# Grouped softmax: tiles of three rows in a ring of four, and one broadcast multiply per row in place of eight scalings

## The chip, the cores and the metric

The kernel runs on one core of one Trainium2 chip. The metric is the device time of that core in microseconds (us), as the median of repeated executions. Beside it stands one execution taken by the hardware profiler, which gives the trace that the profile is read from; its span runs from the first to the last instruction, and its time is a little longer than its span.

## The reference

The input `x` is 4 x 4096 x 4352 in float32. Each row of 4352 values is cut into eight groups of 544, and a softmax is taken over every group:

```python
x_g = x.reshape(B, N, 8, 544)
x_g = x_g - x_g.max(axis=-1, keepdims=True)
exp = np.exp(x_g)
out = exp / exp.sum(axis=-1, keepdims=True)
```

Each value is read once and written once: 285.2 MB come in and 285.2 MB go out, and each element sees one maximum, one exponential with its sum, and one multiply.

## The kernel before, in words

The 16,384 rows lie over 128 partitions, so that each partition handles 128 of them. From here on "row" means one such slot: 128 partitions x 4352 elements, 2.23 MB. `R = 2` rows make a tile (4352 KB), there are 64 tiles, and `NT = 6` buffers hold them in a ring, 12 rows in all. A partition's rows of one tile are adjacent in memory, so that each partition's share of a transfer is one run of 34,816 bytes. The work is done in place: a tile's buffer receives the load, is overwritten by the exponentials and by the scaled values, and is the source of the store.

Three queues work side by side, ordered by semaphores written out by hand:

- SyncE (SP) issues all loads (line 115). From the seventh tile on it first waits until the store out of the same buffer is done (line 114).
- VectorE (DVE) takes, for each row, the negated maxima of the eight groups in one reduction (line 70), and later the reciprocals of the eight sums (line 75) and the eight multiplies, one for each group (line 79). Its order is: maximum of row n+1, then scaling of row n (lines 131 to 134). The first row of a tile waits for the landing of that tile (line 68).
- ScalarE (ACT) computes eight exponentials per row with the sums taken along (line 88), each followed in the trace by a short read of its accumulator. It also issues the stores (line 100).

When a store is issued is set by `LAG = 2`: at tile j, ACT waits for `seen`, which VectorE gives as it takes the landing of tile j, and issues the store of tile j-2 (lines 102 to 108). A tile that is computed waits in its buffer until the second tile after it has landed. The last two stores come without that delay.

The middle of both compute engines' programs is a loop with ten turns of six tiles; the loop heads are placed at a fixed slot of an instruction fetch block (lines 53 to 56). At the end SP waits for the last store of each buffer (lines 116 and 117).

Of the kernel before, what the change touches and what calls it, by code (L numbers as in the profile page):

```python
# [1 line left out]

# [5 lines left out]


@with_exitstack  # L10
def kernel(
    ctx: ExitStack,
    tc: tile.TileContext,
    x: bass.AP,
    out: bass.AP,
):
    nc = tc.nc
    G = 8
    P = 128
    R = 2  # L20
    NT = 6
    S = R * NT
    LAG = 2
    xf = x.flatten_outer_dims()
    of = out.flatten_outer_dims()
    N, D = xf.shape
    Dg = D // G
    nt = N // (P * R)
    turns = (nt - LAG) // NT
    rest = LAG + turns * NT  # L30
    assert rest == nt - 2
    f32 = mybir.dt.float32
    X = mybir.AxisListType.X
    Exp = mybir.ActivationFunctionType.Exp
    xt = xf.rearrange("(t p r) d -> t p (r d)", p=P, r=R)
    ot = of.rearrange("(t p r) d -> t p (r d)", p=P, r=R)
    turn_out = of[:turns * S * P, :].rearrange("(u b p r) d -> u b p (r d)", b=NT, p=P, r=R)

    landed = [tc.alloc_semaphore(f"landed{b}") for b in range(NT)]
    stored = [tc.alloc_semaphore(f"stored{b}") for b in range(NT)]  # L40
    seen = tc.alloc_semaphore("seen")
    max_done = tc.alloc_semaphore("max_done")
    exp_done = tc.alloc_semaphore("exp_done")
    rec_done = tc.alloc_semaphore("rec_done")
    scaled = tc.alloc_semaphore("scaled")

    ctx.enter_context(tc.tile_critical(no_gpsimd_drain=True))  # L47
    bufs = [ctx.enter_context(nc.sbuf_tensor(f"xt{b}", [P, R * D], f32)) for b in range(NT)]
    mx = ctx.enter_context(nc.sbuf_tensor("mx", [P, S, G], f32))
    sm = ctx.enter_context(nc.sbuf_tensor("sm", [P, S, G], f32))  # L50
    rs = ctx.enter_context(nc.sbuf_tensor("rs", [P, S, G], f32))

    def loop(engine):

        return nc.Fori(
            0, turns, engines=OrderedEngineSet([engine.engine]), head_slot={engine.engine: 0})

    def take(engine, sem, n=1):
        engine.sem_inc(sem, -n).wait_op(sem, n, "sem-ge")  # L59

    def row(s):
        b, r = divmod(s, R)
        return bufs[b][:, r * D:(r + 1) * D].rearrange("p (g d) -> p g d", g=G)

    def vector_max(n):
        s = n % S
        if s % R == 0:
            take(nc.vector, landed[s // R], 16)
            nc.vector.sem_inc(seen, 1)
        nc.vector.reduce_max(out=mx[:, s, :], in_=row(s), axis=X, negate=True).then_inc(max_done, 1)  # L70

    def vector_scale(n):
        s = n % S
        take(nc.vector, exp_done)
        nc.vector.reciprocal(out=rs[:, s, :], in_=sm[:, s, :]).then_inc(rec_done, 1)  # L75
        take(nc.vector, rec_done)
        xr = row(s)
        for g in range(G):
            i = nc.vector.tensor_scalar_mul(  # L79
                out=xr[:, g, :], in0=xr[:, g, :], scalar1=rs[:, s, g:g + 1])  # L80
        i.then_inc(scaled, 1)

    def scalar_exp(n):
        s = n % S
        take(nc.scalar, max_done)
        xr = row(s)
        for g in range(G):
            i = nc.scalar.activation(  # L88
                out=xr[:, g, :],
                in_=xr[:, g, :],  # L90
                func=Exp,
                bias=mx[:, s, g:g + 1],
                scale=1.0,
                accum_out=sm[:, s, g:g + 1],
            )
        i.then_inc(exp_done, 1)

    def store(b, target):
        take(nc.scalar, scaled, R)
        nc.scalar.dma_start(out=target, in_=bufs[b][:, :]).then_inc(stored[b], 16)  # L100

    def scalar_tile(j, *targets):

        take(nc.scalar, seen)
        for r in range(R):
            if r < len(targets):
                store((j - LAG + r) % NT, targets[r])
            scalar_exp(j * R + r)


    for t in range(nt):
        b = t % NT
        if t >= NT:
            nc.sync.wait_ge(stored[b], 16 * (t // NT))
        nc.sync.dma_start(out=bufs[b][:, :], in_=xt[t]).then_inc(landed[b], 16)
    for b in range(NT):
        nc.sync.wait_ge(stored[b], 16 * ((nt - b + NT - 1) // NT))


    nc.scalar.preload_act_table(Exp)  # L120
    for j in range(LAG):
        scalar_tile(j)
    with loop(nc.scalar) as u:
        for b in range(NT):
            scalar_tile(LAG + b, turn_out[u, b])
    scalar_tile(nt - 2, ot[nt - 4])
    scalar_tile(nt - 1, ot[nt - 3], ot[nt - 2])
    store((nt - 1) % NT, ot[nt - 1])


    def vector_rows(lo, hi):
        for n in range(lo, hi):
            vector_max(n + 1)
            vector_scale(n)

    vector_max(0)
    vector_rows(0, LAG * R)
    with loop(nc.vector):
        vector_rows(LAG * R, LAG * R + S)
    vector_rows(rest * R, nt * R - 1)  # L140
    vector_scale(nt * R - 1)


# [1 line left out]
_INS = ['x']  # L145
_OUTS = [((4, 4096, 4352), 'float32')]


# [23 lines left out]
```

## Time and profile before

| | us |
|---|---|
| median of 9 runs | 1330.17 |
| lowest and highest | 1329.98, 1332.93 |
| profiled execution, its own time | 1330.27 |
| its span | 1328.5 |
| VectorE busy | 1041.7 |
| ScalarE busy | 764.4 |

The page cuts the span into 40 equal slices and gives for each the busy tenths of every engine and of the 16 DMA engines, with the GB/s that they moved. Its groups name a line, an engine and an operation, then output and input with their shapes, the count, the busy time in us with the mean of one in ns, and behind the second bar the idle time ahead of them and what ended it. Queue 1 carries the loads, queue 10 the stores. In a timeline each line has start, duration (or, where several of a kind are merged, the time from the first to the end of the last), engine, line and count.

### The profile page before, as it was taken

Reading aid. Unit: us, or ns where it says so; the run is one execution under the profiler, and the core shown is the slowest. Engines: PE = TensorE matmul, PEld = TensorE weight load, DVE = VectorE, ACT = ScalarE, POOL = GpSimd, SP = SyncE. Lnnn points to the kernel's source line nnn. Section 1 sums busy time; section 2 is a strip of 40 time slices with the busy share of each in tenths; the row PEclk is TensorE's granted clock in tenths of the full one; section 3 lists DMA queues with packets and bytes.
Section 4 is the critical chain, followed back from the end, with each engine's and each line's share of the span. In section 5 each row is a group of like instructions: output and inputs, shape, how many; then the busy total and the mean of one; then the engine's idle time right before and its main releaser. Section 6 shows DMA issues by size and latency. Waiting matters only on the chain. (4 is left out here: it accounts for less than half of the span.)

```text
span 1328.5 us, 4328 instructions
## 1 busy us (share of the span) xinstructions
DVE 1041.7 (78%) x1280; ACT 764.4 (58%) x2049; POOL 0.2 (0%) x4
## 2 busy tenths in 40 slices
DVE  5899987877877878778787787877878778787781
ACT  3677755655556556565565655655556555565551
POOL 0000000000000000000000000000000000000000
DMA  9999999999999999999999999999999999999997
GB/s 403 418 435 436 434 433 426 434 435 436 436 432 428 433 434 436 436 433 428 432 435 435 436 435 427 431 435 436 435 435 428 432 433 436 436 435 429 430 433 328
DMA packets 18439, 570.49 MB, mean 429 GB/s; under 512 B 2048, under 2 KB 2048, under 8 KB 2048
## 3 DMA queue, kind: packets, MB, share of 16 engines
q1 hardware_dynamic: 9216, 285.22, 49.8%
q10 hardware_dynamic: 9216, 285.22, 49.7%
q14 instruction: 7, 0.06, 0.0%
HBM read 285.21 MB, written 285.21 MB: 429 GB/s over the span
## 5 line engine op out<-in xcount | busy, mean ns | idle before, releaser
L88 ACT ACTIVATE xt<-xt,mx 128x544 f32<-128x544 f32 x1024 | 751.2, 735 | 534.3 <-ACTq L59 534.3
L70 DVE TENSOR_REDUCE mx<-xt 128x8 f32<-128x4352 f32 x128 | 599.2, 4682 | 238.4 <-DVEq L59 235.5
L79 DVE TENSOR_SCALAR xt<-xt,rs 128x544 f32<-128x544 f32 x1024 | 434.1, 498 | 19.2
L88 ACT ACTIVATION_READ_ACCUMULATOR xt<-xt,mx 128x1 f32 x1024 | 191.1, 187 | 0.0
L75 DVE RECIPROCAL rs<-sm 128x8 f32<-128x8 f32 x128 | 24.7, 193 | 4.2 <-DVEq L59 4.2
L120 ACT ACT_TABLE_LOAD x1 | 1.3, 1283 | 0.9 <-SPq L47 0.9
L156 POOL MEMSET const-bfloat16-1.0<- 128x1 bf16 x1 | 0.1, 101 | 0.0
L156 POOL MEMSET const-uint8-127<- 128x1 uint8 x1 | 0.1, 101 | 0.0
L156 POOL MEMSET const-float32-0.0<- 128x1 f32 x1 | 0.1, 98 | 0.2 <-issue 0.2
L156 POOL MEMSET const-float32-1.0<- 128x1 f32 x1 | 0.1, 98 | 0.0
## 6 DMA issues: line engine op xcount, KB each, us to landing
xt<-in_x_dram SPq DMA_DIRECT2D x64, 4352.0 KB, 30.2
out_dram<-xt ACTq DMA_DIRECT2D x64, 4352.0 KB, 51.2
```

The costliest lines, as they stand in the source:

```text
L70: nc.vector.reduce_max(out=mx[:, s, :], in_=row(s), axis=X, negate=True).then_inc(max_done, 1)
L75: nc.vector.reciprocal(out=rs[:, s, :], in_=sm[:, s, :]).then_inc(rec_done, 1)
L79: i = nc.vector.tensor_scalar_mul(out=xr[:, g, :], in0=xr[:, g, :], scalar1=rs[:, s, g:g + 1])
L88: i = nc.scalar.activation(out=xr[:, g, :], in_=xr[:, g, :], func=Exp, bias=mx[:, s, g:g + 1], scale=1.0, accum_out=sm[:, s, g:g + 1],)
L120: nc.scalar.preload_act_table(Exp)
L156: nc = _bacc.Bacc("TRN2", target_bir_lowering=False, num_devices=1)
```

## The change

Tiles become three rows (`R = 3`, 6528 KB) in a ring of four buffers (`NT = 4`), so that the ring still holds 12 rows. 128 rows make 42 tiles of three and a last one of two, 43 in all. The first tile is loaded by three transfers of one row each, each with its own semaphore; the others by one.

The delay of the stores goes: `seen` and `LAG` are gone, and ACT issues the store of tile t right after the exponentials of the first row of tile t+1. Near the end the order is written out: VectorE scales the last row of tile 41 ahead of the maximum of tile 42's first row, and ACT issues the store of tile 41 ahead of the exponentials of that row.

The eight multiplies of a row become one `tensor_tensor` over 4352 elements, whose second input repeats each reciprocal along its group. The loops have ten turns of four tiles, with no slot named for their heads. The final waits follow the order of the stores.

```diff
-    R = 2
-    NT = 6
+    R = 3
+    NT = 4
     S = R * NT
-    LAG = 2
...
+    nr = N // P
+    nt = -(-nr // R)
+    last_rows = nr - (nt - 1) * R
+    turns = (nt - 2) // NT
...
+    first = [tc.alloc_semaphore(f"first{r}") for r in range(1, R)]
-    seen = tc.alloc_semaphore("seen")
...
-    def loop(engine):
-
-        return nc.Fori(
-            0, turns, engines=OrderedEngineSet([engine.engine]), head_slot={engine.engine: 0})
...
         if s % R == 0:
             take(nc.vector, landed[s // R], 16)
-            nc.vector.sem_inc(seen, 1)
+        elif n < R:
+            take(nc.vector, first[n - 1], 16)
...
-        for g in range(G):
-            i = nc.vector.tensor_scalar_mul(
-                out=xr[:, g, :], in0=xr[:, g, :], scalar1=rs[:, s, g:g + 1])
-        i.then_inc(scaled, 1)
+        nc.vector.tensor_tensor(
+            out=xr,
+            in0=xr,
+            in1=rs[:, s, :].unsqueeze(2).to_broadcast([P, G, Dg]),
+            op=mybir.AluOpType.mult,
+        ).then_inc(scaled, 1)
...
-    def scalar_tile(j, *targets):
-
-        take(nc.scalar, seen)
-        for r in range(R):
-            if r < len(targets):
-                store((j - LAG + r) % NT, targets[r])
-            scalar_exp(j * R + r)
+    def store(t, target):
+        take(nc.scalar, scaled, R if t < nt - 1 else last_rows)
+        nc.scalar.dma_start(out=target, in_=tile_of(t)).then_inc(stored[t % NT], 16)
...
+    x0 = xf[:P * R, :].rearrange("(p r) d -> p r d", r=R)
+    for r in range(R):
+        nc.sync.dma_start(out=bufs[0][:, r * D:(r + 1) * D], in_=x0[:, r, :]).then_inc(
+            first[r - 1] if r else landed[0], 16)
+    for t in range(1, nt):
         if t >= NT:
-            nc.sync.wait_ge(stored[b], 16 * (t // NT))
-        nc.sync.dma_start(out=bufs[b][:, :], in_=xt[t]).then_inc(landed[b], 16)
-    for b in range(NT):
-        nc.sync.wait_ge(stored[b], 16 * ((nt - b + NT - 1) // NT))
+            nc.sync.wait_ge(stored[t % NT], 16 * (t // NT))
+        nc.sync.dma_start(out=tile_of(t), in_=dram(xf, t)).then_inc(landed[t % NT], 16)
+    for t in range(nt - NT, nt):
+        nc.sync.wait_ge(stored[t % NT], 16 * (t // NT + 1))
...
+    scalar_exp(0)
+    with nc.scalar.Fori(0, turns) as u:
+        for t in range(NT):
+            for n in range(t * R + 1, t * R + R + 1):
+                scalar_exp(n)
+            store(t, turn_out[u, t])
+    for n in range(turns * S + 1, nr):
+        if n == (nt - 1) * R:
+            store(nt - 2, dram(of, nt - 2))
+        scalar_exp(n)
+        if n == (nt - 2) * R:
+            store(nt - 3, dram(of, nt - 3))
+    store(nt - 1, dram(of, nt - 1))
...
+    lead = R - 1
     vector_max(0)
-    vector_rows(0, LAG * R)
-    with loop(nc.vector):
-        vector_rows(LAG * R, LAG * R + S)
-    vector_rows(rest * R, nt * R - 1)
-    vector_scale(nt * R - 1)
+    vector_rows(0, lead)
+    with nc.vector.Fori(0, turns):
+        vector_rows(lead, lead + S)
+    vector_rows(lead + turns * S, (nt - 1) * R - 1)
+    vector_scale((nt - 1) * R - 1)
+    vector_max((nt - 1) * R)
+    vector_rows((nt - 1) * R, nr - 1)
+    vector_scale(nr - 1)
```

## The prediction

> **What bounds the kernel now.** I read the page first: the slices, the queues, the groups.
>
> ```profile
> DVE  5899987877877878778787787877878778787781
> ACT  3677755655556556565565655655556555565551
> DMA  9999999999999999999999999999999999999997
> q1 hardware_dynamic: 9216, 285.22, 49.8%
> q10 hardware_dynamic: 9216, 285.22, 49.7%
> L88 ACT ACTIVATE xt<-xt,mx 128x544 f32<-128x544 f32 x1024 | 751.2, 735 | 534.3 <-ACTq L59 534.3
> L70 DVE TENSOR_REDUCE mx<-xt 128x8 f32<-128x4352 f32 x128 | 599.2, 4682 | 238.4 <-DVEq L59 235.5
> L79 DVE TENSOR_SCALAR xt<-xt,rs 128x544 f32<-128x544 f32 x1024 | 434.1, 498 | 19.2
> ```
>
> The DMA engines are busy in every slice; loads and stores take equal halves, 99.5% together. VectorE idles 238.4 us, nearly all ahead of its maxima, that is, waiting for landings. So transfers set the time, and a change can act in three places only: the time of a pass of bytes, the start, and the end, if the DMA then lacks work. The chain of work is no help: it stops at VectorE's last multiplies at 1303, while the stores run on.
>
> Next, the timelines: SP's loads, ACT's first store, the last two stores, and VectorE at the end.
>
> ```profile
> 609.66 41.47 SPq L115 DMA_DIRECT2D xt<-in_x_dram  x3
> 1228.63 21.01 SPq L115 DMA_DIRECT2D xt<-in_x_dram  x2
> 48.92 5.47 ACTq L100 DMA_DIRECT2D out_dram<-xt  x1
> 1289.02 0.34 ACTq L100 DMA_DIRECT2D out_dram<-xt  x1
> 1303.59 0.34 ACTq L100 DMA_DIRECT2D out_dram<-xt  x1
> 1177.18 4.68 DVE L70 TENSOR_REDUCE mx<-xt 128x8 f32<-128x4352 f32 x1 [4.10 <-DVEq L59]
> 1181.78 0.19 DVE L75 RECIPROCAL rs<-sm 128x8 f32<-128x8 f32 x1
> 1182.12 3.40 DVE L79 TENSOR_SCALAR xt<-xt,rs 128x544 f32<-128x544 f32 x8
> 1185.44 4.68 DVE L70 TENSOR_REDUCE mx<-xt 128x8 f32<-128x4352 f32 x1
> 1280.58 4.68 DVE L70 TENSOR_REDUCE mx<-xt 128x8 f32<-128x4352 f32 x1 [4.10 <-DVEq L59]
> ```
>
> Loads go out every 20.57 us in the middle ((41.47 - 0.33)/2) and every 20.68 us at the end. In that time two rows come in and two go out, so a pass of one row in one direction costs 20.68/4 = 5.17 us; I use 5.16. VectorE's starts give 4.60 for a maximum, 0.34 from reciprocal to multiply and 3.32 for eight multiplies, 8.26 a row. Last, the end in windows (busy time of the three engines with counts, clock, DMA share, GB/s):
>
> ```profile
> 1315.00:1320.00 5.00, 0.00 (x0) 0.00 (x0) 0.00 (x0) 1.00 0.90 390
> 1320.00:1325.00 5.00, 0.00 (x0) 0.00 (x0) 0.00 (x0) 1.00 0.11 49
> ```
>
> The DMA runs full until 1319.4; in finer windows single packets of one or two slower engines follow until 1325.0, and the span ends 3.5 us later. The DMA thus never lacks work, and the reason is a store backlog. Call the rows landed but not yet stored the **lead**. The load issued at 1249.3 needed store 57, done some 1.8 us earlier (as 1325.0 stands to SP's release at 1326.8): 116 rows stored, and 124.9 landed, since VectorE takes tile 62 at 1259.90. Lead 8.9. At the last landing, 1280.0, 8.9 rows make 46 us of stores, to 1326 (seen: 1325.0), and the last store, issued at 1303.59, joins a queue that still has work.
>
> **The Trainium skill.** "VectorE: DVE Perf Modes", the perf-mode tier table, gives float32 `tensor_scalar` two elements per cycle and `tensor_tensor` one. The trace agrees for the first: 3.32/8 = 415 ns for 544 elements, below the 567 ns that one per cycle at 0.96 GHz needs; it has none of the second. "Vector Engine (DVE) Microarchitecture Reference", measured stream behaviour, gives 1.0417 ns per column plus about 75 ns: 4.61 us for 4352, and the maximum shows 4.60. "DMA: Bandwidth & Descriptors", queues, rings and completion order, says that an engine takes turns between its queues packet by packet, as the equal halves show; where 436 GB/s comes from, same page, has 27.2 GB/s per port, so that 34,816 bytes need 1.280 us, against 20.68/16 = 1.2925 here.
>
> **The change, part by part.**
>
> *Multiply.* Eight for 3.32 us become one of 4.61 us (estimate from that slope; it can't be less, one-element rate being the operation's best). A row costs VectorE 4.60 + 0.34 + 4.61 = 9.55, a tile 28.7. Its DMA period is 6 x 5.16 = 31.0, so 2.3 us a tile stay as cover and the steady state costs nothing. Upper end for the multiply: the same section has 1.73 ns per column where a source hops every element, and no case of a repeated float32 (the modes section has a repeated 2-byte element at one per cycle); that is a rival below.
>
> *Fewer, larger transfers.* 128 become 45 loads + 43 stores = 88, so packets per engine fall from 1024 to 704 for the same bytes. Above 1.280 us each packet costs 12.5 ns. If all of that goes with packets and completions, 320 x 12.5 ns = 4.0 us are saved; if with bytes, nothing. I take -1.8.
>
> *First tile by rows.* SP issues two more transfers, about 0.4 us each, behind which only loads wait that queue for a busy DMA: 0. VectorE starts after one row, at 8.8 instead of 14.03, but the loads run without a break until the ring is full either way: 0 in itself.
>
> *Loop heads.* At loop entry VectorE branched at 50.4 and went on at 56.3, with 2.9 us of idle that the page calls issue. That goes, or comes back on ACT at a turn (its body stays above 200 instructions): about 5.5 us ahead of an exponential that VectorE needs some 3 us after its earliest end. The rest comes out of the 2.3 us a tile: 0, and if that cover is gone, 2 to 3 us once.
>
> *Final waits.* Three waits within 0.1 us: -0.1 at most.
>
> *No delay of the stores, and the ring.* This sets the lead. A load alone shows the offset: issued at 0.95, last packets at 13.4, which is 8 x 1.286 + 2.1, so data start at 3.0. After: maximum 0 ends 13.4, maximum 1 18.5 (row 1 lands at 13.3, noticed 0.6 later), exponentials 0 end 19.6 (6.1 from the trace), scaling 0 24.5, maximum 2 29.1, scaling 1 34.1, maximum 3 (tile 1 lands at 33.9) 39.1, scaling 2 44.0, exponentials 3 45.3. Store 0 goes out at 45.4, its data at 47.5. By then (47.5 - 3)/5.16 = 8.6 rows are in. The other 3.4 last until 82.4 at half rate; store 0 ends at 78.5, and 1.8 + 2.1 later load 4 flows, at 82.4. Lead 8.6, kept from then on. If ACT's first issue again takes 5.47 us, 9.6 rows are in, but loads run dry at 77.3 and load 4 flows at 84.3: the stores catch up 7.0/5.16 = 1.4 rows, lead 8.25. The same reckoning for before gives 10.3 less 1.3 = 9.0, measured 8.9. I take 8.4. On ACT the store's wait for the scaling stands ahead of the next row's exponentials: that scaling ends 10.2 after the tile's landing, the exponentials in front of the wait 11.4, so nothing is held, nor at the end, where store 41 goes out 4.5 ahead of the maximum that exponentials 126 need.
>
> *The end, from the landing of tile 41* (three rows; VectorE at +0.6): maxima 123 to 125 and scalings 122 to 124 end at +29.3; exponentials 125 start after maximum 125 (+24.3) and end at +30.5; scaling 125 ends +35.4 and store 41 goes out. Maxima 126 and 127 end at +44.6, exponentials 126 at +46.2, scaling 126 at +51.1, exponentials 127 at +52.2, scaling 127 at +57.2. Store 42 goes out at +57.3, data at +59.4. Until then the DMA has the load of two rows and the lead: (8.4 + 2) x 5.16 = 53.7. It stands still for **5.7 us**; then two rows pass, 10.3 us, and the close is as before. Ends: 4.6 with lead 8.6, about 7.4 with 8.25 and the 1 us by which the reckoning ran long above. In the old kernel the same point comes at 1303.6 + 2.1, 20 us before its stores run out: three rows behind a slower scaling, with less lead, use that up.
>
> Sum on the profiled execution: 1330.27 + 5.7 - 1.8 - 0.1 = 1334.1; it lies 0.1 above the median, so **1334.0**.
>
> **Rivals.**
>
> *The stores still cover the end.* Something early holds the stores back, the lead stays above 9.5, (9.5 + 2) x 5.16 = 59.3, no gap: 1330.2 - 1.9 = 1328.3, not slower. For it: ACT's issue of 5.47 us, and fetch pauses. Against: the ring. At a store's end 9 rows can be in beside it, and the next load needs 3.9 us to flow, so a lead above 9 - 3.9/10.3 = 8.6 is worked off.
>
> *Per-packet cost is larger than the trace lets me see.* If larger packets saved over 3 us of the 5.7, the result is within 0.2%; over 8.4 us would make it faster, but the whole excess of before over the port rate is only 1024 x 12.5 ns = 12.8 us, and 31% of the packets go. Time 1330 to 1331.
>
> *VectorE becomes the bound.* It does from 31.0/3 = 10.3 us a row, that is from a multiply of 5.4 us (1.22 ns per element). At 1.73 ns it takes 7.6 and a row 12.5: 128 x 12.5 + 35 for both ends = about 1640. For it: a repeated float32 is not measured. Against: the 2-byte case.
>
> *Fetches at every turn* of ACT's loop, all on one slow DMA engine, say ten of 1 us: about 1344.
>
> **How the numbers follow.** The gap opens, 80%: +5.7 (4.6 to 7.4) less 0 to 4.0, own range 1330.7 to 1337.7. Stores cover, 8%. A large saving per packet, 5%. VectorE bound, 4%. Fetches, 3%. The range 1330.2 to 1338.3 leaves out the last two, the covered case and half of the savings, 17 in 100. 0.2% is 2.7 us, about what a measurement can tell from no change. Of the 80, 56 lie above 1332.8 and 24 within; of the covered cases, 5 within and 3 faster; of the saving, 2 within and 3 faster; the last two, 7, are slower: slower 63, same 31, faster 6.
>
> **What would show it.** Right: loads every 31 us; the multiply near 4.6 us; the last but one store issued some 35 us after tile 41's landing and the last some 57; DMA share near zero for about 5 us ahead of the last store's data. Wrong: full DMA windows up to the last byte (the lead), a landing of the last tile earlier than 1280 by more than 4 us (packets), VectorE without idle ahead of its maxima (multiply). Weakest is the lead, a difference of two large counts: one row is 5 us.

## The result, and the profile after

The changed kernel takes 1339.11 us (median of 10 runs, 1335.96 to 1346.66) against 1330.20 (30 runs) for the kernel before: ratio 1.0076 [1.0065, 1.0088], which compares means. By the medians it is 8.9 us slower. Forecast were 1334.0 and a range that ended at 1338.3. Two more executions are on record, at 1348.70 and 1353.31 us, outside the ten; over all twelve the median would be 1340.6. The one at 1348.7 (span 1346.9) is the profiled one, 9.6 us above the median: its trace shows what happens, and the sizes have to come from the experiments.

From the page of the changed kernel: three rows of slices, the two queues, and the three groups that answer to those shown before.

```profile
DVE  6998999999988999999999989999999999998995
DMA  9999999999999999999999999999999999999977
GB/s 408 402 380 438 431 434 433 431 436 430 437 430 437 430 433 434 434 434 431 437 425 434 434 430 437 425 442 425 430 434 428 433 430 434 434 431 434 433 301 306
q1 hardware_dynamic: 6480, 285.22, 49.5%
q10 hardware_dynamic: 6192, 285.22, 49.1%
L90 ACT ACTIVATE xt<-xt,mx 128x544 f32<-128x544 f32 x1024 | 751.2, 734 | 563.5 <-ACTq L55 563.5
L70 DVE TENSOR_REDUCE mx<-xt 128x8 f32<-128x4352 f32 x128 | 599.1, 4681 | 103.2 <-DVEq L55 103.2
L78 DVE TENSOR_TENSOR xt<-xt,rs 128x4352 f32<-128x4352 f32 x128 | 600.6, 4692 | 18.8
```

The middle of the kernel still belongs to the DMA: it is busy in every slice, and VectorE still idles 103.2 us ahead of its maxima, although the multiply has gone from 434.1 to 600.6 us. The rate, about 433 GB/s in the middle, is low in two places: slices 2 and 3 (33.7 to 101 us) and the last two.

The end in its timelines: VectorE (start, duration, operation, idle time ahead), SP's last load, ACT's first store and last three.

```profile
44.53 2.08 ACTq L102 DMA_DIRECT2D out_dram<-xt  x1
1250.90 4.69 DVE L78 TENSOR_TENSOR xt<-xt,rs 128x4352 f32<-128x4352 f32 x1
1255.51 4.68 DVE L70 TENSOR_REDUCE mx<-xt 128x8 f32<-128x4352 f32 x1
1261.25 0.33 SPq L113 DMA_DIRECT2D xt<-in_x_dram  x1
1277.05 4.69 DVE L70 TENSOR_REDUCE mx<-xt 128x8 f32<-128x4352 f32 x1 [2.36 <-DVEq L55]
1286.78 0.35 ACTq L102 DMA_DIRECT2D out_dram<-xt  x1
1312.20 0.35 ACTq L102 DMA_DIRECT2D out_dram<-xt  x1
1333.91 0.34 ACTq L102 DMA_DIRECT2D out_dram<-xt  x1
```

The multiply takes 1255.51 - 1250.90 = 4.61 us. Tile 41 lands 0.6 us before VectorE takes it, at 1276.4; store 41 follows 35.8 us later and store 42 57.5 us later. The forecast was 35.4 and 57.3.

The last stretch in windows of 4 us (busy time of VectorE, ScalarE and GpSimd with counts, clock, DMA share, GB/s):

```profile
1300.00:1304.00 4.00, 3.85 (x3) 3.06 (x9) 0.00 (x0) 1.00 0.59 250
1304.00:1308.00 4.00, 2.57 (x3) 2.90 (x8) 0.00 (x0) 1.00 0.06 26
1308.00:1312.00 4.00, 4.00 (x1) 0.00 (x0) 0.00 (x0) 1.00 0.03 13
1312.00:1316.00 4.00, 4.00 (x2) 0.00 (x0) 0.00 (x0) 1.00 0.98 418
...
1328.00:1332.00 4.00, 3.09 (x2) 0.62 (x2) 0.00 (x0) 1.00 0.00 0
1332.00:1336.00 4.00, 1.80 (x1) 0.00 (x0) 0.00 (x0) 1.00 0.32 139
```

The DMA stands still twice. The second time, for 4.0 + 0.68 x 4 = 6.7 us ahead of store 42, is the one forecast. The first, ahead of store 41, was not: 0.41, 0.94 and 0.97 of three windows, 9.3 us. A share of 0.06 is one engine of the 16 working alone. A window counts a packet whole where it starts, and a packet of 52,224 bytes takes 1.9 us here, so such sums are good to about 1 us; from the packets' own start and end times the first gap is 9.2 us and the second 6.2.

Last, the minute in which the first stores come in among the loads. Before:

```profile
48.00:108.00 60.00, 56.09 (x71) 41.44 (x111) 0.00 (x0) 1.00 1.00 425
```

and after, the whole and three parts of it:

```profile
48.00:108.00 60.00, 58.97 (x21) 37.22 (x100) 0.00 (x0) 1.00 1.00 386
60.00:66.00 6.00, 6.00 (x2) 4.51 (x14) 0.00 (x0) 1.00 0.93 313
72.00:78.00 6.00, 5.85 (x4) 2.42 (x7) 0.00 (x0) 1.00 1.11 374
78.00:84.00 6.00, 6.00 (x2) 5.60 (x16) 0.00 (x0) 1.00 0.84 331
```

The engines count as busy and yet move 386 GB/s instead of 425. At 434 GB/s those bytes take 60 x 386/434 = 53.4 us, so 6.6 us go by here, against 1.2 in the kernel before. The load of tile 4 went out at 87.6, where the prediction's reckoning gives about 80.3. The lead at the end is lower too: the load issued at 1261.25 needed store 38, done some 1.8 us earlier, so 117 rows were stored, and with tile 40 in at 1245.4 and tile 41 at 1276.4, 123 + 3 x 14.0/31.0 = 124.4 had landed. Lead 7.4; I took 8.4. Whether the slow minute is what lowered it is looked at below.

### The profile page after: what moved, and what is told of

It reads as the page before. It is cut to its first block, busy times and chain, and to the rows that moved or that the text cites. A ratio compares the mean times of both kernels' runs of the same rounds, so it can differ in the third digit from the quotient of the medians.

```text
span 1346.9 us, 3181 instructions
## 1 busy us (share of the span) xinstructions
DVE 1207.0 (90%) x384; ACT 764.3 (57%) x2049; POOL 0.2 (0%) x4
## 5 line engine op out<-in xcount | busy, mean ns | idle before, releaser
L70 DVE TENSOR_REDUCE mx<-xt 128x8 f32<-128x4352 f32 x128 | 599.1, 4681 | 103.2 <-DVEq L55 103.2
L78 DVE TENSOR_TENSOR xt<-xt,rs 128x4352 f32<-128x4352 f32 x128 | 600.6, 4692 | 18.8
```

What stands on the lines that cost most here:

```text
L78: nc.vector.tensor_tensor(out=xr, in0=xr, in1=rs[:, s, :].unsqueeze(2).to_broadcast([P, G, Dg]), op=mybir.AluOpType.mult,).then_inc(scaled, 1)
```

## The experiments

The theory after the result: the DMA's standing still at the end costs what the prediction says, and slow mixing of large packets at the start costs the rest, directly and through a row of lead. The rival is that the end alone is worse than I reckoned.

**Only the multiply, in the kernel before.**

```diff
-        for g in range(G):
-            i = nc.vector.tensor_scalar_mul(out=xr[:, g, :], in0=xr[:, g, :], scalar1=...)
+        nc.vector.tensor_tensor(out=xr, in0=xr, in1=rs[...].to_broadcast([P, G, Dg]), op=mult)
```

> The kernel before with its eight scalings replaced by the one multiply, nothing else. If the multiply is covered, as predicted, VectorE's last row ends about 5 us later, the DMA still has stores for 10 us or more then, and the time is within 0.1% of before, 1329 to 1331.5. If a row of 9.55 us eats into the body: slower by more than 2.7 us.

Measured 1329.71 (1329.49 to 1329.94), ratio 0.9995 [0.9987, 1.0004]. The multiply alone costs nothing that can be measured: the DMA covers it, at the end of the kernel before as well.

**Only the multiply undone, in the changed kernel.**

```diff
-        nc.vector.tensor_tensor(out=xr, in0=xr, in1=rs[...].to_broadcast([P, G, Dg]), op=mult)
+        for g in range(G):
+            i = nc.vector.tensor_scalar_mul(out=xr[:, g, :], in0=xr[:, g, :], scalar1=...)
```

> The changed kernel with the eight scalings per row in place of the one multiply. Tail theory without the lead: the last chain shortens by 5 us, time about 1334. Tail theory with the lead: the first store also goes out some 5 us earlier, which costs a row of lead and gives 5 us back: 1337 to 1340. A body bound by VectorE would gain more than 5 us.

Measured 1333.62 (1326.66 to 1341.64), ratio 1.0017 [1.0003, 1.0031]: 5.5 us below the changed kernel by the medians. With eight scalings of 3.32 us the chain at the end is shorter: the last two stores go out 31.9 and 52.3 us after the landing of tile 41, in place of 35.8 and 57.5. In the profiled execution (span 1325.2) the DMA stands still once, for 0.41 of 4 us:

```profile
1308.00:1312.00 4.00, 2.88 (x7) 0.00 (x0) 0.00 (x0) 1.00 0.59 252
1312.00:1316.00 4.00, 0.00 (x0) 0.00 (x0) 0.00 (x0) 1.00 0.98 418
```

So the slower multiply, free in the steady state, is paid for at the end. But the 22 times fall into two groups, 9 between 1326.7 and 1329.7 and 13 from 1332.8 up; I return to that below.

**Smaller tiles, R = 2 and NT = 6, with everything else of the change.**

```diff
-    R = 3
-    NT = 4
+    R = 2
+    NT = 6
...
-        if n == (nt - 2) * R:
-            store(nt - 3, dram(of, nt - 3))
+        t = n // R - 1
+        if n % R == 0 and turns * NT <= t <= nt - 3:
+            store(t, dram(of, t))
```

> The changed kernel with tiles of two rows in a ring of six, all else as changed (one multiply per row, no delay of the stores, first tile by rows). Lead theory: the first store goes out at about 35 us, so the lead is only 6.6 rows, the last chain from the landing of tile 62 to the last byte is 58 us; the landing comes at 3 + (252 - 6.6) x 5.16 = 1269, the time is about 1333. Rival (large transfers lose time in the body because the 16 engines drift apart): the body runs at 5.14 to 5.17 us a pass with no drift and the time is at or below 1330.

Measured 1332.33 (1331.80 to 1332.71), ratio 1.0015 [1.0009, 1.0022]. The lead, reckoned as above, came out as expected at 6.6, and the last tile but one landed at 1269.1 (expected 1269). The time is near the 1333 of the lead theory, where the rival had at most 1330. The run says more: packets of 34,816 bytes mix at 435 GB/s from 48 to 108 us, and the spread shrinks to 0.9 us.

**The last two tiles stored row by row**, first in the changed kernel, then with R = 2.

```diff
+    def store_row(t, r):
+        rows = R if t < nt - 1 else last_rows
+        take(nc.scalar, scaled)
+        nc.scalar.dma_start(out=dram(of, t).rearrange("p (r d) -> p r d", r=rows)[:, r, :],
+                            in_=bufs[t % NT][:, r * D:(r + 1) * D]).then_inc(stored[t % NT], 16)
...
+        elif (nt - 2) * R < n < (nt - 1) * R:
+            store_row(nt - 2, n - 1 - (nt - 2) * R)
+        elif n > (nt - 1) * R:
+            store_row(nt - 1, n - 1 - (nt - 1) * R)
```

> The changed kernel, but the stores of its last two tiles go out row by row, each as soon as its row is scaled. Tail theory (the DMA stands still near the end because VectorE's last rows come late and the lead is only some 7.4 rows): after the landing of tile 41 the DMA has work for 33 us, then rows 123 to 125 are there in time, row 126 comes at +51, row 127 at +57, last byte at +62 in place of +67: 5 us less than the changed kernel, about 1334 us. Rival (the time was lost in the body, in the transfers themselves, and the end only follows): within 1.5 us of the changed kernel, 1337.5 to 1340.5.

Measured 1335.50 (1330.67 to 1349.29), ratio 1.0053 [1.0025, 1.0080]. The direction is the one expected, -3.6 us, but the interval overlaps that of the changed kernel: alone this settles nothing. Its trace settles something else, the lead:

```profile
48.00:108.00 60.00, 58.97 (x21) 37.19 (x100) 0.00 (x0) 1.00 0.99 386
1237.29 4.69 DVE L70 TENSOR_REDUCE mx<-xt 128x8 f32<-128x4352 f32 x1 [2.19 <-DVEq L55]
1259.96 0.33 SPq L120 DMA_DIRECT2D xt<-in_x_dram  x1
```

The minute is as slow as in the changed kernel, and the load of tile 4 goes out at 87.5. But with the last load issued at 1259.96 and tile 40 in at 1236.7, the reckoning gives a lead of 8.1. So a slow minute does not by itself cost a row of lead.

> The two-row, six-buffer version of the changed kernel with the stores of its last two tiles by row. Tail theory: of the 58 us from the landing of tile 62 to the last byte 3 to 4 us go, since row 126 can leave while row 127 is computed; 1332.3 becomes about 1329. Rival (the two-row version is slower than before for another reason than the end): stays within 1 us of 1332.3.

Measured 1328.70 (1328.31 to 1329.06), ratio 0.9979 [0.9965, 0.9994]: 3.6 us below the same kernel with whole stores. Here, where the spread is small, the end's cost is shown. This version beats both kernels, the one before by 1.5 us.

**The first tile as one transfer.**

```diff
-    for r in range(R):
-        nc.sync.dma_start(out=bufs[0][:, r * D:(r + 1) * D], in_=x0[:, r, :]).then_inc(
-            first[r - 1] if r else landed[0], 16)
-    for t in range(1, nt):
+    for t in range(nt):
```

> The changed kernel with its first tile in one transfer. Lead theory: the first store goes out some 10 us later, near 55, the lead rises until the ring caps it, to about 8.3 rows in place of 7.4; time 4 to 5 us less than the changed kernel, near 1334. Rival (the split first tile does nothing, as I predicted, and the lead is set by the ring alone): within 1.5 us of the changed kernel. If the slow transfers between 50 and 105 us come from the three small loads, they vanish here, and another 5 us with them.

Measured 1342.26 (1335.64 to 1346.70), ratio 1.0078 [1.0054, 1.0103]. A miss: 1334 was expected. The lead at the end was 8.1, near the 8.3 expected, but the first store now goes out at 54.9 and the second at 83.5, the loads run dry in between, and the DMA has half a window without work:

```profile
78.00:84.00 6.00, 5.85 (x4) 5.53 (x15) 0.00 (x0) 1.00 0.52 200
```

From the changed kernel it can't be told apart. What the gap at the start costs was not separated from the rest.

**All transfers of a tile cut in two**, so that packets have 26,112 bytes: in the changed kernel, in the same with eight scalings, and (17,408 bytes) in the kernel before.

```diff
-        nc.sync.dma_start(out=tile_of(t), in_=dram(xf, t)).then_inc(landed[t % NT], 16)
+        w = (R if t < nt - 1 else last_rows) * D // 2
+        for h in range(2):
+            nc.sync.dma_start(out=tile_of(t)[:, h * w:(h + 1) * w],
+                              in_=dram(xf, t)[:, h * w:(h + 1) * w]).then_inc(landed[t % NT], 16)
```

(the stores likewise)

> The changed kernel with every transfer of a tile cut into two, each with half of every partition's bytes (26,112 in place of 52,224); tiles, ring and order stay. Packet theory (packets of 52 KB make transfers slow between 50 and 105 us and let single DMA engines fall behind by up to 17 us): both vanish, the lead is 8.4, the landing of tile 41 near 1259, the end 72 us later, about 1331, with a spread of 2 us like that of the two-row kernels. Rival (the ring of four large tiles leaves the queues too thin, whatever the packets): as the changed kernel, 1336 to 1347 with that spread.

Measured 1336.54 (1334.57 to 1336.66), ratio 1.0044 [1.0031, 1.0058]. The rate from 48 to 108 us went to 428 GB/s, the lead to 8.3 and the spread from 10.7 to 2.1 us, as expected; the time stayed 5.5 above the 1331 expected.

> The changed kernel with both the halved transfers and the eight scalings per row. Packet theory: only the fast group of the eight-scalings kernel is left, 1326.5 to 1329, faster than before, since no store waits at the end. Rival (thin queues): two groups again, near 1327 and 1335.

Measured 1332.15 (1330.95 to 1332.98), ratio 1.0014 [1.0007, 1.0020]. Of the two groups of the uncut kernel one is left, but 5 us above the lower. Both misses have one sign and size, which pointed to the price of a packet.

> The kernel before with every transfer cut into two (17,408 bytes per partition, 256 transfers of a tile's halves in place of 128). It prices a packet: 1024 packets more per engine and twice the completions. If the 12.5 ns above the port rate went with packets, as the upper end of my estimate had it: 12.8 us slower, 1343. At the 5.6 ns that I took: 1336. If the excess goes with bytes: 1330 to 1331.

Measured 1336.44 (1335.45 to 1336.58), ratio 1.0040 [1.0026, 1.0054]: +6.2 us for 128 x 8 = 1024 more packets per engine, 6.1 ns each, completions included. The 680 more packets of the two cut versions cost 4.1 us by that. Without them they are at 1332.4 and 1328.0, near the 1331 and within the 1326.5 to 1329 expected.

**The kernel with eight scalings run twice more**, the same code as in its run above, to see what parts its two groups.

> The eight-scalings kernel again, one look, for its two groups of times. If the group is set by the transfers between 48 and 78 us: a time under 1329 goes with rates near 435 GB/s there and a lead of 8.4 at the end, a time above 1332 with rates under 400 GB/s and a lead at or below 7.6. If it is set by a DMA engine that falls behind later, the rates there are alike in both.

> The same once more: under 1329 with rates near 435 GB/s between 48 and 78 us and lead 8.4, or above 1332 with rates under 400 GB/s and lead 7.6 or less; the other theory has the rates there alike in both groups.

The first took 1326.77, the second 1333.61, one in each group. Windows of the first:

```profile
48.00:108.00 60.00, 58.48 (x75) 43.47 (x117) 0.00 (x0) 1.00 0.97 421
60.00:66.00 6.00, 5.85 (x7) 3.72 (x11) 0.00 (x0) 1.00 1.05 454
```

and of the second:

```profile
48.00:108.00 60.00, 55.72 (x69) 41.37 (x112) 0.00 (x0) 1.00 0.99 382
60.00:66.00 6.00, 5.85 (x7) 3.72 (x11) 0.00 (x0) 1.00 0.95 323
```

In the part shown both engines do the same work, instruction for instruction, and the DMA is busy in both; it moves 454 GB/s in one and 323 in the other. Over the minute, 39 GB/s less are 60 x 39/434 = 5.4 us, of the 6.8 between the two. The load of tile 4 goes out at 80.6 in the first and 87.6 in the second, and the lead is 8.4 against 7.9. For the second I had expected 7.6 at most, a miss: here the slow minute goes with only half a row of lead. The two differ already at ACT's first store, whose issue takes 1.42 us in the first and 3.61 in the second. Of the kernels with the same start, 2.08 and 2.02 went with 386 GB/s, 1.52 with 423. Whether that is a cause or a sign was not tested.

**Only the first four tiles' transfers cut in two**, the first turn being written out ahead of the loops. This adds 56 packets per engine, 0.3 us.

```diff
+        w = R * D // 2 if t < NT else tile_of(t).shape[1]
+        for lo in range(0, tile_of(t).shape[1], w):
+            nc.sync.dma_start(out=tile_of(t)[:, lo:lo + w], in_=dram(xf, t)[:, lo:lo + w]
+                              ).then_inc(landed[t % NT], 16)
...
+    for t in range(NT):
+        for n in range(t * R + 1, t * R + R + 1):
+            scalar_exp(n)
+        store(t, dram(of, t), half=True)
```

> The changed kernel with only the transfers of its first four tiles cut into halves (26,112 bytes), and its first turn written out ahead of the loops; all later transfers keep 52,224 bytes. If the loss beyond the prediction lies in the slow mixing of large packets while the first stores run (some 6.7 us between 48 and 108 us, and the row of lead that goes with it): 1332.4, within 1.5 us, with rates near 430 GB/s there and a lead of 8.4. If large packets lose time throughout (an engine that falls behind by 10 us or more): 1336 or more, with the spread of the changed kernel. Halves cost 24 x 2 packets x 6 ns here, nothing.

Measured 1333.71 (1332.36 to 1341.74), ratio 1.0036 [1.0022, 1.0051], within 1332.4 ± 1.5 and below the rival's 1336. Its windows, at the start and at the end:

```profile
48.00:108.00 60.00, 58.98 (x21) 36.88 (x99) 0.00 (x0) 1.00 1.00 425
1292.00:1296.00 4.00, 3.89 (x1) 0.00 (x0) 0.00 (x0) 1.00 0.15 65
1296.00:1300.00 4.00, 4.00 (x2) 0.00 (x0) 0.00 (x0) 1.00 0.97 418
...
1308.00:1312.00 4.00, 4.00 (x1) 4.00 (x13) 0.00 (x0) 1.00 0.98 420
1312.00:1316.00 4.00, 3.04 (x3) 1.33 (x4) 0.00 (x0) 1.00 0.03 13
1316.00:1320.00 4.00, 2.51 (x1) 0.00 (x0) 0.00 (x0) 1.00 0.32 139
...
1328.00:1332.00 4.00, 0.00 (x0) 0.00 (x0) 0.00 (x0) 1.00 0.33 139
```

The early rate is back, and the lead is 8.1. The DMA still stands still twice: for 0.85 x 4 = 3.4 us ahead of store 41, which goes out at 1296.91, and for (0.97 + 0.68) x 4 = 6.6 us ahead of store 42. So what this kernel mends is the first minute, and the first gap at the end only shrinks. Cutting 7 of the 88 transfers goes with 5.4 us less than the changed kernel. Its first turn also stands outside the loops, which was not tried alone; but the version with all transfers cut keeps the loops and has its early rate back as well (428), so the cut is the likely cause. Three of the nine times (1335.84, 1337.46 and 1341.74) still lie late.

## Why the prediction was wrong

*Fewer, larger transfers* failed. It bounded the term from nothing to 4.0 us saved and took -1.8. The saving was sized right: at 6.1 ns, 320 packets per engine are 2.0 us, within what the cut kernel before shows. What it left out is a loss. Packets of 52,224 bytes, three rows of a partition in one run, can mix badly while the first stores come in among the loads: 386 GB/s in the profiled execution, 382 in one later run, against 425 before, 435 with R = 2 and 421 to 428 where packets were cut or mixing went well. With those of the first turn cut the time is 5.4 us lower, which is what carried the result out of the range, and it has a sign that no bound of mine allowed. The rate in the middle, which I had read for this term, shows nothing of it. Nor do the equal halves of loads and stores, which follow from equal bytes, show how well the two mix.

*No delay of the stores, and the ring* was right in its mechanism and nearly in its size: 8.4 was forecast, and the reckoning gives 8.1 to 8.4 in three kernels with a good first minute, 8.1 and 7.9 in two traces with a slow one. The 7.4 of the profiled execution goes with a late engine instead. The trace has the completions of the 16 parts of each load. The last part came 0.3 us behind the last but one at 126 us, 5.0 us at 746 and 9.6 at tile 41; for the same load it is 3.6 us in the kernel with the mended first turn, and 4.6 near 1239 in the kernel before. A tile counts as landed with its last part, so this engine lowers a lead that is counted in tiles; counted in packets, the same moment has 8.7 rows. The prediction's care about ACT's first issue was needless; that took 2.08 us and not 5.47.

*The end* had its chain right to 0.4 us, and the gap ahead of store 42 nearly: 5.7 was forecast, and it is 6.6 where the lead is 8.1. Two other terms were wrong. The first is the gap ahead of store 41, which I priced at nothing. Without its own three rows, what is left there is (lead - 3 + 2) x 5.16: 38.2 us at lead 8.4, just past the +37.5 at which I let its data start. The data in fact start sooner. In finer windows of the profiled execution the first packets after the issues of store 41 (1312.20) and store 42 (1333.91) start here:

```profile
1312.80:1313.00 0.20, 0.20 (x1) 0.00 (x0) 0.00 (x0) 1.00 0.00 0
1313.00:1313.20 0.20, 0.20 (x1) 0.00 (x0) 0.00 (x0) 1.00 9.21 3917
1334.40:1334.60 0.20, 0.00 (x0) 0.00 (x0) 0.00 (x0) 1.00 0.00 0
1334.60:1334.80 0.20, 0.00 (x0) 0.00 (x0) 0.00 (x0) 1.00 2.83 1219
```

That is 0.7 to 1.0 us after the issue, not 2.1, so about +36.7 for store 41. At lead 8.1 the work left is 36.6 us and no gap should open, yet the kernel with the mended first turn has 3.4 us and the profiled execution 9.3. The reckoning treats the 16 engines as one. In both traces some are still at work while the rest have run dry, in the profiled execution one alone from 1304 to 1308; that the late engine makes this gap is argued, not shown. The execution is 9.6 us above the median, so the median should have less of it.

The second is the close, which I took "as before". In the kernel before 9.1 us pass from the end of full DMA at 1319.4 to the end of the span, with a few engines still working. (The 1325.0 given there is a start: one more packet starts just after it and runs to about 1326.3.)

```profile
1325.00:1326.00 1.00, 0.00 (x0) 0.00 (x0) 0.00 (x0) 1.00 0.08 35
```

In the kernel with the mended first turn store 42 flows from 1318.7 for 10.3 us, to 1329.0, and the span ends at 1331.6: 2.6 us. So 6.5 us that the prediction kept are gone.

*Multiply* and the rival in which VectorE becomes the bound: settled. A repeated float32 costs 4.61 us, and the multiply alone is free; at the end, under three-row tiles, it costs some 4 to 7 us: 1333.7 with a mended first turn against 1326.7 to 1329.7 in the lower group with eight multiplies. *Loop heads* and *First tile by rows*, both at nothing, were not separated from the rest: one transfer for the first tile changed the start in two ways at once.

The forecast of 1334.0 lies beside the 1333.7 of the kernel with a mended first turn, and that is in part luck: the gap left out and the close kept nearly cancel. With the terms as that trace has them, 1330.2 + 3.4 + 6.6 - 6.5 - 2.0 + 0.3 for its extra packets gives 1332.0; 1.7 us stay without an account. The slow mixing is then the 5.4 us up to 1339.1. That is a difference of two medians, but two other readings agree in size: 5.4 us from the rates of the two later runs with eight scalings, and 6.6 in the profiled execution.

Of the rivals none came true. That the stores still cover the end is refuted by the windows. Fetches at every turn are not on the page, which has 4 packets of instructions for the whole span:

```profile
q14 instruction: 4, 0.03, 0.0%
```

Two things stay open: why large packets mix badly at first, and only in some executions of the same code, and why one DMA engine falls behind, and further in some executions than in others.

## What to carry to other kernels

In a kernel that the DMA bounds, count how many rows of stores stand in the queue when the last load lands, and compare that with the compute chain from there to each of the last stores, not only to the last one; where it falls short, store the last tiles in smaller pieces, which gave 3.6 us here for a few lines. Leave some room in that count, since the engines do not end together. A larger packet saves a few ns, so look at the first mixing of loads and stores and at the spread of the times before taking it: tiles of two rows with stores by row at the end gave 1328.7 with a spread of 0.8 us.

## What the runs showed of the hardware

- Packets of 52,224 bytes moved between 382 and 423 GB/s in the first minute of mixed loads and stores; two executions of the same code had 382 and 421, with whole times of 1333.6 and 1326.8 us. Packets of 34,816 bytes moved 425 and 435.
- A packet with its completion costs about 6.1 ns of an engine's time (1024 more per engine, +6.2 us).
- A DMA engine that counts as busy need not move bytes at its rate: over that minute a share of 0.99 went with 382 GB/s and one of 0.97 with 421.
- The 16 DMA engines do not keep step. At tile 41 of the profiled execution the last part of the load came 9.6 us behind the last but one, after 0.3 us at 126 us; near 1239 us of the kernel before it was 4.6.
- With the DMA idle, the first packets of a store started 0.7 to 1.0 us after its issue (two stores).
- A float32 operand that repeats each of eight values 544 times cost 4.61 us for 4352 elements, 1.06 ns per element, as much as a maximum over as many (4.60).
